# Seven-product sums in the words' own place, two word buffers, later transposes and four kept ring pieces

## The chip, the cores and the metric

The kernel runs on one core of a Trainium2 chip. The metric is the device time of one execution in microseconds (us). The engines of the core work side by side and wait for each other through semaphores: TensorE (PE; PEld is its weight load) multiplies matrices, VectorE (DVE) and ScalarE (ACT) do elementwise work, GpSimd (POOL) a little of it, and SyncE (SP) issues the loads from HBM in the order of one queue.

## The reference

An encoder of two layers works on 256 tokens of width 2048, all in fp32. Each layer adds a mixer and a gated feed-forward block (FFN), each followed by a layer norm:

```python
for layer in range(DEPTH):
    y = ab_mixer(...) if layer % 2 == 0 else cd_mixer(...)
    x = layer_norm(alpha * x + y, ...)
    y = (silu(x @ w_gate) * (x @ w_up)) @ w_down   # hidden width 5632
    x = layer_norm(alpha * x + y, ...)
```

Layer 0 mixes with a neighbourhood attention and a gated recurrence (`ab`), layer 1 with a multi-scale pool and a grouped-query attention (`cd`). Every mixer ends in an output projection. The change concerns the FFN and its borders.

## The kernel before

**Products.** An fp32 product is made of three matmuls in the faster F32R format (`mm3`, L261 to L266). Both factors are split into a high part and a remainder: ScalarE casts (`hi`, L122), VectorE subtracts (`lo`, L123). TensorE then adds low by high, high by high and high by low into one PSUM bank. Activations are split once and lie transposed (`xT`, `yT`); weights are split as they arrive. `load_half` (L143) loads 512 KB into one of four `raw` buffers; the split goes to a ring of `whi` and `wlo` buffers, which `open_ring` lengthens in some stages. A half feeds 12 matmuls of 512 columns: two token tiles, two rows of weights, three matmuls each.

**The FFN** (`ffn`, L462 to L527). The hidden width is 11 chunks of 512. Chunk 0 is made directly (`whole`). Chunks 1 to 10 are made by `unit`, in three phases that hold chunks 0 to 2, 3 to 6 and 7 to 10. Behind each phase the down projection of its chunks runs as four quarters `n`, and its result is added to the residual `res`.

**A unit** (L417 to L460) makes gate and up of one chunk from eight pairs of weight rows, in the order `PAIRS`. Five pairs are plain: two halves, 24 matmuls. Three (`SEVEN`: 5, 6, 7) use a seven-product scheme for the 2 by 2 block of token tiles and gate/up columns, 21 matmuls instead of 24. `load_seven` (L398) loads such a pair as one word of 1 MB (`rs`). From its four pieces come seven factors: three pieces are used as they are (cast L406, subtraction L410), four are sums, made in a tile `z` (L407 to L409) and split in their turn (L122, L123). `SEVEN_ORDER` gives the order of the seven products and the bank of each. The activations' counterparts are made once per layer by `forms_of` (`fs`, split into `fmh` and `fml`).

At the end of a unit ScalarE and VectorE combine the eight banks (L444 to L454), VectorE multiplies the gate by the up part into `g` (L458), and for each token tile TensorE transposes `g` (`transpose4`, L119), whose result is split into `yTh` and `yTl`: the down projection's left factor.

**PSUM** has eight banks. In the mixers they are "uses": three `acc`, two `tr` for transposes, three `mx`. In the FFN's units and first two down projections they are two "sides" of four, which change places from unit to unit.

**Order.** A scheduler sets the order of each engine's instructions from the program; `tc.high_priority` moves a block ahead by an offset. SP's loads go out in one queue's order, each as soon as its buffer is free. At the end of an FFN the norm runs with the last quarter of the down projection: `norm` scales `res` (L309), and `flip` transposes it for the next stage in pieces laid between the next stage's matmuls.

Of the kernel before, what the change touches and what calls it, by code (L numbers as in the profile page):

```python
# [11 lines left out]
F32 = mybir.dt.float32  # L12
# [6 lines left out]
P = 128  # L19
# [51 lines left out]
PAIRS = (0, 1, 5, 2, 3, 6, 4, 7)  # L71
SEVEN = (5, 6, 7)


@with_exitstack
def trunk(ctx: ExitStack, tc: tile.TileContext, a, out):
# [94 lines left out]

    def mm_chunk(halves, lhs, outs, tok_major=False, after=None, before=None):
# [32 lines left out]
        else:  # L205
            for i, (src, _) in enumerate(halves):
                loaded.append(load_half(src, before(i) if before else ()))
                for tok in range(NT):
                    mms(i, tok)
            if after:  # L210
# [36 lines left out]
    def transpose4(src, hi, lo):  # L247
# [4 lines left out]
        split(hi, lo, v)  # L252
# [19 lines left out]
    def residual_tools(res, gam, bet, betT):  # L272
        stats = [sm.tile([P, 4, 6], F32, tag=f"st{t}", name=f"st{t}", bufs=1) for t in range(NT)]
# [82 lines left out]
    def out_proj(w, order, groups, res, gb):  # L356
        evac, norm = residual_tools(res, *gb)
# [16 lines left out]
    def forms_of(sp, xT):  # L374
# [3 lines left out]
        xs = sp.tile([P, NT, 2 * n, P], F32, tag="rs", name="xs", bufs=1)  # L378
# [4 lines left out]
        fs = sp.tile([P, 4, n, P], F32, tag="z", name="fs", bufs=1)  # L383
# [14 lines left out]
    def load_seven(sp, src):  # L398

        with tc.high_priority(offset=400):  # L400
            raw = sp.tile([P, 4, NCH], F32, tag="rs", name="rs", bufs=1)
            hi = sp.tile([P, 7, NCH], F32R, tag="sh", name="sh", bufs=2)
            lo = sp.tile([P, 7, NCH], F32R, tag="sl", name="sl", bufs=2)
            z = sp.tile([P, 4, NCH], F32, tag="z", name="z", bufs=1)
            last_load[0] = nc.sync.dma_start(raw, src).ins
            nc.scalar.copy(hi[:, :3], raw[:, :3])  # L406
            nc.vector.tensor_tensor(z[:, :2], raw[:, 0:3:2], raw[:, 3:4].to_broadcast([P, 2, NCH]), op=add)  # L407
            nc.vector.tensor_tensor(z[:, 2], z[:, 0], raw[:, 2], op=add)
            nc.vector.tensor_tensor(z[:, 3], z[:, 2], raw[:, 1], op=add)  # L409
            nc.vector.tensor_tensor(lo[:, :3], raw[:, :3], hi[:, :3].bitcast(F32), op=sub)  # L410
            split(hi[:, 3:], lo[:, 3:], z)
# [3 lines left out]
    SEVEN_ORDER = ((0, "11", "p1"), (5, "f", "p6"), (3, "e", "p5"), (4, "g", "p7"), (1, "12", "c11"), (2, "h", "c12"), (6, "22", "c21"))  # L415

    def unit(sp, w, lhs, forms, yT):  # L417
# [8 lines left out]
        sevens = [p for p in PAIRS if p in SEVEN]  # L426
# [658 lines left out]
```

## Time and profile before

| what | value |
|---|---|
| median of 3 runs | 2236.31 us (2235.67 to 2237.08) |
| profiled execution | 2237.32 us |
| its span, first to last instruction | 2235.5 us |
| mean granted clock of TensorE | 0.988 |
| busy: PE, PEld, DVE, ACT | 98%, 81%, 73%, 48% |
| loaded and stored | 420.63 MB, 188 GB/s |

A share of busy time is a mean over stages. Matmuls are pipelined and overlap in the trace, so a busy PE is not PE at its peak. What a stage costs is read from TensorE's waits there and from the granted clock, which falls to half for some microseconds behind some of them.

### The profile page before, as it was taken

To read this page: it belongs to the slowest core of one execution; us is meant where nothing else is said; L and a number is where in the kernel's file an instruction comes from. 1 tells how busy PE (TensorE), PEld (TensorE's weight loads), DVE (VectorE), ACT (ScalarE), POOL (GpSimd) and SP (SyncE) were. 2 spreads that over 40 slices of the span, in tenths; PEclk is the share of its full clock that TensorE was granted. 3 is DMA by queue.
4 is the path that set the end of the run, shared out by engine and by line. 5 is a ranking of instruction groups with operands and counts; after the bars stand their busy time and mean duration, and the time that the engine had idled before them with its cause. 6 is when DMAs were issued, how large, how long until landed. Compare 5 with 4: busy or idle time off the path is not lost.

```text
span 2235.5 us, 26590 instructions
## 1 busy us (share of the span) xinstructions
PE 2183.4 (98%) x10000; PEld 1806.8 (81%) x10000; DVE 1636.4 (73%) x2016; ACT 1073.3 (48%) x1280; POOL 80.4 (4%) x67
## 2 busy tenths in 40 slices
PE   8999999999999999999999899999999999999997
PEld 7888888887778888888878688877778888888876
DVE  6886687566886788848876586675885789568865
ACT  6445544445453455544544564463544555345542
POOL 0010001002000000000000200020000000000001
PEclk9999999999999999999999999999999999999999
DMA  8555545664556555655557363654655556655553
GB/s 294 159 160 183 175 129 185 234 226 142 188 173 214 188 197 193 205 186 198 190 179 243 110 229 121 220 173 153 218 190 195 179 188 216 206 188 190 189 200 121
DMA packets 110257, 420.63 MB, mean 188 GB/s; under 512 B 13488, under 2 KB 16048, under 8 KB 101168
## 3 DMA queue, kind: packets, MB, share of 16 engines
q1 hardware_dynamic: 110128, 418.93, 56.0%
q8 instruction: 78, 1.28, 0.2%
q14 instruction: 51, 0.42, 0.1%
HBM read 416.78 MB, written 2.10 MB: 187 GB/s over the span
## 4 chain that ended last, share of the span: by engine, by line
PE 89%; DVE 6%; DMA 2%; issue 2%; ACT 1%; SPq 0%; POOL 0%; DVEq 0%; ACTq 0%; POOLq 0%
PE acc L264 39%; PE bside L264 25%; PE aside L264 21%; DVE wlo L123 2%; DMA rs<-in_gu 2%; PE mx L663 1%; PE mx L264 1%; PE tr L119 1%; DVE sl L410 1%; ACT whi L122 0%; PE aside L119 0%; PE bside L119 0%; DVE xTl L340 0%; ACT sh L406 0%; PE mx L709 0%
## 5 line engine op out<-in xcount | busy, mean ns | idle before, releaser
L123 DVE TENSOR_TENSOR wlo<-raw,whi 128x1024 fp32r<-128x1024 f32 (+1 forms) x641 | 787.6, 1238 | 383.5 <-ACT whi L122 379.2
L122 ACT CAST whi<-raw 128x1024 fp32r<-128x1024 f32 (+1 forms) x641 | 670.7, 1051 | 732.8 <-PE acc L264 266.1
L264 PE MATMUL acc<-whi,xTl 128*128 128x512 f32 x800 | 319.4, 400 | 14.4 <-DVE xTl L340 8.0
L264 PE MATMUL acc<-wlo,xTh 128*128 128x512 f32 x800 | 315.2, 396 | 5.1 <-DVE wlo L123 3.9
L264 PE MATMUL acc<-whi,xTh 128*128 128x512 f32 x800 | 317.1, 396 | 0.0
L264 PE MATMUL acc<-whi,yTl 128*128 128x512 f32 x512 | 201.3, 394 | 0.1
L264 PE MATMUL acc<-whi,yTh 128*128 128x512 f32 x512 | 200.7, 392 | 0.0
L264 PE MATMUL acc<-wlo,yTh 128*128 128x512 f32 x512 | 198.6, 391 | 0.0
L264 PEld LDWEIGHTS acc<-whi,xTl 128*128 128x128 f32 x800 | 152.4, 190 | 46.0 <-DVE xTl L340 8.5
L264 PEld LDWEIGHTS acc<-wlo,xTh 128*128 128x128 f32 x800 | 151.9, 190 | 39.0 <-DVE wlo L123 6.8
L264 PEld LDWEIGHTS acc<-whi,xTh 128*128 128x128 f32 x800 | 152.5, 191 | 29.1
L264 PE MATMUL bside<-whi,xTl 128*128 128x512 f32 x400 | 157.2, 394 | 1.4 <-DVE g L445 1.4
L264 PE MATMUL aside<-whi,xTl 128*128 128x512 f32 x400 | 156.0, 391 | 1.2 <-DVE yTl L123 1.2
L264 PE MATMUL bside<-whi,xTh 128*128 128x512 f32 x400 | 156.9, 392 | 0.0
L264 PE MATMUL aside<-whi,xTh 128*128 128x512 f32 x400 | 155.7, 389 | 0.0
L264 PE MATMUL bside<-wlo,xTh 128*128 128x512 f32 x400 | 153.5, 393 | 0.0
L264 PE MATMUL aside<-wlo,xTh 128*128 128x512 f32 x400 | 153.5, 390 | 0.0
L406 ACT CAST sh<-rs 128x1536 fp32r<-128x1536 f32 x60 | 89.0, 1484 | 131.9 <-DMA rs<-in_gu 77.7
L123 DVE TENSOR_TENSOR sl<-z,sh 128x2048 fp32r<-128x2048 f32 x60 | 137.3, 2288 | 20.6 <-ACT sh L122 19.5
L122 ACT CAST sh<-z 128x2048 fp32r<-128x2048 f32 x60 | 114.7, 1911 | 74.4 <-DVE z L409 74.4
L410 DVE TENSOR_TENSOR sl<-rs,sh 128x1536 fp32r<-128x1536 f32 x60 | 105.2, 1754 | 40.6 <-ACT sh L406 40.4
L264 PEld LDWEIGHTS acc<-wlo,yTh 128*128 128x128 f32 x512 | 96.8, 189 | 20.7 <-DVE wlo L123 0.5
(255 smaller groups left out, 3505.1 us busy)
## 6 DMA issues: line engine op xcount, KB each, us to landing
raw<-in_gu SPq DMA_DIRECT2D x232, 512.0 KB, 4.2
raw<-in_down SPq DMA_DIRECT2D x176, 512.0 KB, 4.2
raw<-in_ab_in SPq DMA_DIRECT2D x127, 512.0 KB, 4.2
rs<-in_gu SPq DMA_DIRECT2D x60, 1024.0 KB, 5.2
raw<-in_cd_in SPq DMA_DIRECT2D x40, 512.0 KB, 4.2
raw<-in_ab_out SPq DMA_DIRECT2D x32, 512.0 KB, 4.4
raw<-in_cd_out SPq DMA_DIRECT2D x32, 512.0 KB, 4.1
x<-in_xT SPq DMA_DIRECT2D x8, 256.0 KB, 6.4
```

Source lines behind the costliest of these rows:

```text
L119: return nc.tensor.transpose(o, src, eye)
L122: nc.scalar.copy(hi, src)
L123: nc.vector.tensor_tensor(lo, src, hi.bitcast(F32), op=sub)
L264: ins = nc.tensor.matmul(o, lhs[a], rhs[b], start=start and n == 0, stop=stop and n == 2)
L406: nc.scalar.copy(hi[:, :3], raw[:, :3])
L410: nc.vector.tensor_tensor(lo[:, :3], raw[:, :3], hi[:, :3].bitcast(F32), op=sub)
L663: nc.tensor.matmul(m[:, 2 * h + s, :], kk[:, h, s * P : (s + 1) * P], qq[:, h, r * P : (r + 1) * P], start=True, stop=True,)
```

## The change

1. In `load_seven` the first three pieces are split first, and then the sums overwrite the word itself (`raw`); the tile `z` is gone. The words have two buffers, which the forms use first (`xs`, `fs`). `SEVEN_ORDER` puts the three products of the first split ahead and the sixth (`f`) late.
2. Unit 1 takes its pairs in the order `PAIRS_FIRST`: four plain pairs ahead of the first word. Words have a lower priority in the first unit of each phase (`EARLY_FIRST`).
3. The product `g` and its transposes are no longer queued at the end of the unit: `later` holds each set of transposes, and `half_done` lets it go after two or three further halves, with the split at high priority. Behind unit 10 they go to `tr` banks within the down projection.
4. The end stage's ring of seven pieces becomes four and three. The four are `kept`: they stay through the `cd` mixer, in place of its own four (`wcd`), and into layer 1's output projection.
5. The norm's parameters are loaded behind the first quarter of the last down projection.

```diff
@@ -69,7 +69,11 @@
 PHASES = ((0, 1, 2), (3, 4, 5, 6), (7, 8, 9, 10))
 
 PAIRS = (0, 1, 5, 2, 3, 6, 4, 7)
+PAIRS_FIRST = (0, 1, 2, 3, 5, 4, 6, 7)
 SEVEN = (5, 6, 7)
+
+EARLY = 400
+EARLY_FIRST = 150
 
 
 @with_exitstack
@@ -169,6 +173,16 @@
     def two(k):
         return k, k + 1
 
+
+    later = []
+
+    def half_done(n=1):
+        for entry in list(later):
+            entry[0] -= n
+            if entry[0] <= 0:
+                later.remove(entry)
+                entry[1]()
+
     def mm_chunk(halves, lhs, outs, tok_major=False, after=None, before=None):
 
         n = len(halves)
@@ -207,6 +221,7 @@
                 loaded.append(load_half(src, before(i) if before else ()))
                 for tok in range(NT):
                     mms(i, tok)
+                half_done()
             if after:
                 for tok in range(NT):
                     after(tok)
@@ -244,12 +259,13 @@
         return f
 
 
-    def transpose4(src, hi, lo):
+    def transpose4(src, hi, lo, ahead_by=0):
         t = trp()
         for k in range(4):
             transpose(t[:, k * P : (k + 1) * P], src[:, k * P : (k + 1) * P], ident)
         v = t.rearrange("p (k t) -> p k t", k=4)
-        split(hi, lo, v)
+        with tc.high_priority(offset=ahead_by):
+            split(hi, lo, v)
 
     def split_tile(pool, shape, src, tag, bufs=1):
         hi = pool.tile(shape, F32R, tag=tag + "h", name=tag + "h", bufs=bufs)
@@ -269,8 +285,10 @@
         return pair[0][ix], pair[1][ix]
 
 
-    def residual_tools(res, gam, bet, betT):
-        stats = [sm.tile([P, 4, 6], F32, tag=f"st{t}", name=f"st{t}", bufs=1) for t in range(NT)]
+    def new_stats():
+        return [sm.tile([P, 4, 6], F32, tag=f"st{t}", name=f"st{t}", bufs=1) for t in range(NT)]
+
+    def residual_tools(res, gam, bet, betT, stats):
 
         def evac(tok, n, psum, start, last):
             r = res[tok][:, n * NCH : (n + 1) * NCH]
@@ -354,7 +372,7 @@
 
 
     def out_proj(w, order, groups, res, gb):
-        evac, norm = residual_tools(res, *gb)
+        evac, norm = residual_tools(res, *gb, new_stats())
         lhs = y_lhs(groups)
         xT = new_xT()
         for n in range(4):
@@ -375,12 +393,12 @@
 
         n = len(SEVEN)
         k = [slice(2 * SEVEN[0] + e, 2 * SEVEN[0] + 2 * n, 2) for e in range(2)]
-        xs = sp.tile([P, NT, 2 * n, P], F32, tag="rs", name="xs", bufs=1)
+        xs = sp.tile([P, NT, 2 * n, P], F32, tag="rs", name="xs", bufs=2)
         for t in range(NT):
             s = slice(2 * SEVEN[0], 2 * SEVEN[0] + 2 * n)
             nc.vector.tensor_tensor(xs[:, t], xT[0][t][:, s, :].bitcast(F32), xT[1][t][:, s, :].bitcast(F32), op=add)
         x11, x12, x21, x22 = (xs[:, t, e : 2 * n : 2, :] for t in range(2) for e in range(2))
-        fs = sp.tile([P, 4, n, P], F32, tag="z", name="fs", bufs=1)
+        fs = sp.tile([P, 4, n, P], F32, tag="rs", name="fs", bufs=2)
         e, f, g, h = (fs[:, i] for i in range(4))
         nc.vector.tensor_tensor(e, x22, x21, op=sub)
         nc.vector.tensor_tensor(f, e, x11, op=add)
@@ -395,26 +413,24 @@
             out.append({"11": x(0, k1), "12": x(0, k2), "22": x(1, k2), "e": e, "f": f, "g": g, "h": h})
         return dict(zip(SEVEN, out))
 
-    def load_seven(sp, src):
-
-        with tc.high_priority(offset=400):
-            raw = sp.tile([P, 4, NCH], F32, tag="rs", name="rs", bufs=1)
-            hi = sp.tile([P, 7, NCH], F32R, tag="sh", name="sh", bufs=2)
-            lo = sp.tile([P, 7, NCH], F32R, tag="sl", name="sl", bufs=2)
-            z = sp.tile([P, 4, NCH], F32, tag="z", name="z", bufs=1)
+    def load_seven(ss, sp, src, early):
+
+        with tc.high_priority(offset=early):
+            raw = sp.tile([P, 4, NCH], F32, tag="rs", name="rs", bufs=2)
+            hi = ss.tile([P, 7, NCH], F32R, tag="sh", name="sh", bufs=2)
+            lo = ss.tile([P, 7, NCH], F32R, tag="sl", name="sl", bufs=2)
             last_load[0] = nc.sync.dma_start(raw, src).ins
-            nc.scalar.copy(hi[:, :3], raw[:, :3])
-            nc.vector.tensor_tensor(z[:, :2], raw[:, 0:3:2], raw[:, 3:4].to_broadcast([P, 2, NCH]), op=add)
-            nc.vector.tensor_tensor(z[:, 2], z[:, 0], raw[:, 2], op=add)
-            nc.vector.tensor_tensor(z[:, 3], z[:, 2], raw[:, 1], op=add)
-            nc.vector.tensor_tensor(lo[:, :3], raw[:, :3], hi[:, :3].bitcast(F32), op=sub)
-            split(hi[:, 3:], lo[:, 3:], z)
+            split(hi[:, :3], lo[:, :3], raw[:, :3])
+            nc.vector.tensor_tensor(raw[:, 0:4:3], raw[:, 0:3:2], raw[:, 3:4].to_broadcast([P, 2, NCH]), op=add)
+            nc.vector.tensor_tensor(raw[:, 2], raw[:, 0], raw[:, 2], op=add)
+            nc.vector.tensor_tensor(raw[:, 1], raw[:, 2], raw[:, 1], op=add)
+            split(hi[:, 3:], lo[:, 3:], raw)
         return lambda i: (hi[:, i, :], lo[:, i, :])
 
 
-    SEVEN_ORDER = ((0, "11", "p1"), (5, "f", "p6"), (3, "e", "p5"), (4, "g", "p7"), (1, "12", "c11"), (2, "h", "c12"), (6, "22", "c21"))
-
-    def unit(sp, w, lhs, forms, yT):
+    SEVEN_ORDER = ((0, "11", "p1"), (1, "12", "c11"), (2, "h", "c12"), (3, "e", "p5"), (6, "g", "p7"), (5, "f", "p6"), (4, "22", "c21"))
+
+    def unit(ss, sp, pairs, w, lhs, forms, yT, opening):
 
         b = {n: side_bank() for n in ("c11", "c21", "c12", "c22")}
         begun = set()
@@ -423,13 +439,13 @@
             mm3(b[name], x, wt, name not in begun, last)
             begun.add(name)
 
-        sevens = [p for p in PAIRS if p in SEVEN]
-        plain = [p for p in PAIRS if p not in SEVEN]
-        for p in PAIRS:
+        sevens = [p for p in pairs if p in SEVEN]
+        plain = [p for p in pairs if p not in SEVEN]
+        for p in pairs:
             if p in SEVEN:
                 if p == sevens[0]:
                     b.update((n, side_bank(True)) for n in ("p1", "p6", "p5", "p7"))
-                wt = load_seven(sp, w[p])
+                wt = load_seven(ss, sp, w[p], EARLY_FIRST if opening else EARLY)
                 for i, x, name in SEVEN_ORDER:
                     product(name, forms[p][x], wt(i), p == sevens[-1])
             else:
@@ -439,6 +455,7 @@
                         for kk in range(2):
                             name = f"c{tok + 1}{n + 1}"
                             product(name, lhs(tok, ks[kk]), (hi[:, kk, :], lo[:, kk, :]), name == "c22" and p == plain[-1] and kk == 1)
+                    half_done()
         with tc.high_priority(offset=1000):
             g0, w_, v, x = (sp.tile([P, NCH], F32, tag=n, name=n, bufs=1) for n in ("g0", "g1", "u0", "u1"))
             nc.scalar.copy(g0, b["p1"])
@@ -457,9 +474,9 @@
             for tok, (g, u) in enumerate(((g0, v), (w_, x))):
                 nc.vector.tensor_tensor(g, g, u, op=mult)
                 s = slice(tok * P, (tok + 1) * P)
-                transpose4(g, yT[0][:, :, s], yT[1][:, :, s])
-
-    def ffn(layer, xT, res, mix_pool, close_mix, last):
+                later.append([2 + tok, lambda g=g, s=s: transpose4(g, yT[0][:, :, s], yT[1][:, :, s], 1000)])
+
+    def ffn(layer, xT, res, mix_pool, close_mix, keep, last):
         lhs = x_lhs(xT)
         w = a[f"gu{layer}"]
 
@@ -487,7 +504,7 @@
         groups = {0: whole(0, mix_pool, True)}
         close_mix()
         stack = ExitStack()
-        sp = later_pool(stack, f"s{layer}")
+        ss, sp = later_pool(stack, f"ss{layer}"), later_pool(stack, f"sp{layer}")
         open_banks("sides")
         with tc.high_priority(offset=2000):
             forms = forms_of(sp, xT)
@@ -497,19 +514,20 @@
             for c in chunks:
                 if c not in groups:
                     groups[c] = new_yT()
-                    unit(sp, w[c], lhs, forms, groups[c])
+                    unit(ss, sp, PAIRS_FIRST if c == 1 else PAIRS, w[c], lhs, forms, groups[c], c - 1 in (0, *(p[0] - 1 for p in PHASES)))
             gl = [groups[c] for c in chunks]
             if end:
                 stack.close()
                 open_banks("uses")
-                open_ring(later_pool(stack, f"er{layer}"), 7)
-                fp = later_pool(stack, f"e{layer}")
-                gb = load_gb(fp, layer, "ffn")
+                open_ring(keep(f"er{layer}"), 4)
+                open_ring(later_pool(stack, f"e{layer}"), 3)
+                fp = later_pool(stack, f"g{layer}")
                 nxt = None if last else new_xT()
-                evac, norm = residual_tools(res, *gb)
-            else:
-                evac, _ = residual_tools(res, None, None, None)
+            stats = new_stats()
+            evac, norm = residual_tools(res, None, None, None, stats)
             for n in range(4):
+                if end and n == 1:
+                    evac, norm = residual_tools(res, *load_gb(fp, layer, "ffn"), stats)
                 outs = [acc() for _ in range(NT)]
                 halves = [(a[f"down{layer}"][n, 2 * c + i], two(4 * ci + 2 * i)) for ci, c in enumerate(chunks) for i in range(2)]
 
@@ -522,8 +540,9 @@
                 mm_chunk(halves, y_lhs(gl), outs, tok_major=(end and n == 3), after=after)
             if not end:
                 banks["side"] ^= 1
-        rings.pop()
-        stack.close()
+        if end:
+            rings.pop()
+            stack.close()
         return nxt
 
 
@@ -947,27 +966,32 @@
     def later_pool(stack, name):
         return stack.enter_context(tc.tile_pool(name=name, bufs=1, reuse_waits="tile"))
 
+
+    kept = ExitStack()
+
+    def keep(name):
+        return later_pool(kept, name)
+
     def layer_end(i, w, groups, yT, last):
 
         stack = ExitStack()
-        open_ring(later_pool(stack, f"fr{i}"), 7)
+        open_ring(later_pool(stack, f"fr{i}"), 7 - 4 * i)
         fp = later_pool(stack, f"f{i}")
 
         def close():
-            rings.pop()
+            del rings[1:]
             stack.close()
+            kept.close()
 
         xT = out_proj(w, groups, yT, res, load_gb(fp, i, "mix"))
-        return ffn(i, xT, res, fp, close, last)
+        return ffn(i, xT, res, fp, close, keep, last)
 
     xT = layer_end(0, a["ab_out"], AB_OUT_GROUPS, yT, False)
     yT = [new_yT() for _ in range(4)]
-    with tc.tile_pool(name="wcd", bufs=1, reuse_waits="tile") as wcd:
-        rings.append((wcd, 4))
-        with tc.tile_pool(name="cd", bufs=1, reuse_waits="tile") as mp:
-            cd_mixer(mp, xT, yT)
-    rings.pop()
+    with tc.tile_pool(name="cd", bufs=1, reuse_waits="tile") as mp:
+        cd_mixer(mp, xT, yT)
     layer_end(1, a["cd_out"], CD_OUT_GROUPS, yT, True)
+    kept.close()
 
 
 
```

The new line numbers: `split` is L126 and L127, `mm3` L280, the transposes L123, the sums L424 to L426, the combination at a unit's end L461 to L475. Three places show how the instructions move.

SP, layer 0's FFN, from chunk 0 into units 1 and 2 (`raw` are halves, `rs` the words). Before:

```order
L159 DMA raw<-in_gu 128x1024 x24
L405 DMA rs<-in_gu 128x2048
L159 DMA raw<-in_gu 128x1024
L405 DMA rs<-in_gu 128x2048
L159 DMA raw<-in_gu 128x1024 x3
L405 DMA rs<-in_gu 128x2048
L159 DMA raw<-in_gu 128x1024 x4
L405 DMA rs<-in_gu 128x2048
L159 DMA raw<-in_gu 128x1024 x2
L405 DMA rs<-in_gu 128x2048
L159 DMA raw<-in_gu 128x1024 x2
L159 DMA raw<-in_down 128x1024 x3
```

Now:

```order
L163 DMA raw<-in_gu 128x1024 x24
L422 DMA rs<-in_gu 128x2048 x2
L163 DMA raw<-in_gu 128x1024 x5
L422 DMA rs<-in_gu 128x2048
L163 DMA raw<-in_gu 128x1024
L422 DMA rs<-in_gu 128x2048
L163 DMA raw<-in_gu 128x1024 x4
L422 DMA rs<-in_gu 128x2048 x2
L163 DMA raw<-in_gu 128x1024 x2
L163 DMA raw<-in_down 128x1024 x3
L422 DMA rs<-in_gu 128x2048
L163 DMA raw<-in_down 128x1024 x5
```

The first two words go out together, and five halves follow before the third; two pairs of words stand together where there were single ones.

TensorE, layer 0, from the last matmuls of unit 10 (`aside`, `bside`) to the last down projection (`acc`). Before:

```order
L264 MATMUL bside<-sh,xTh_3815 128x512
L264 MATMUL bside<-sl,xTh_3815 128x512
L119 MATMUL bside<-ident,g_9104 128x128 x4
L119 MATMUL bside<-ident,g_9105 128x128 x4
L264 MATMUL acc<-whi,yTl 128x512
L264 MATMUL acc<-whi,yTh 128x512
L264 MATMUL acc<-wlo,yTh 128x512
L264 MATMUL acc<-whi,yTl 128x512
```

Now, the same border, and then the place of the first set of transposes:

```order
L280 MATMUL bside<-sh,xTh_3815 128x512
L280 MATMUL aside<-sl,fmh 128x512 x3
L280 MATMUL bside<-sl,xTh_3815 128x512
L280 MATMUL acc<-whi,yTl 128x512
L280 MATMUL acc<-whi,yTh 128x512
L280 MATMUL acc<-wlo,yTh 128x512
L280 MATMUL acc<-whi,yTl 128x512
```

```order
L280 MATMUL acc<-whi,yTl 128x512
L280 MATMUL acc<-whi,yTh 128x512
L280 MATMUL acc<-wlo,yTh 128x512
L123 MATMUL tr<-ident,g_9077 128x128 x4
L280 MATMUL acc<-whi,yTl 128x512
L280 MATMUL acc<-whi,yTh 128x512
L280 MATMUL acc<-wlo,yTh 128x512
```

The transposes have moved from between the two stages to behind 24 matmuls of the second, into a `tr` bank; the second set follows 12 matmuls later.

ScalarE, layer 0, from the last down projection (the first row holds its halves) into the norm (`res`), the flips (`xTh`) and the first halves of the `cd` projection. Before:

```order
L122 CAST whi<-raw 128x1024 x28
L309 ACTIVATE res_3796<-res_3796,rstd 128x512 x4
L338 ACTIVATE xTh_9152<-tr,betT 128x128 x4
L338 ACTIVATE xTh_9152<-mx,betT 128x128 x4
L122 CAST whi<-raw 128x1024 x2
L338 ACTIVATE xTh_9152<-tr,betT 128x128 x4
L338 ACTIVATE xTh_9152<-mx,betT 128x128 x4
L122 CAST whi<-raw 128x1024 x2
L309 ACTIVATE res_3797<-res_3797,rstd 128x512 x3
```

Now:

```order
L126 CAST whi<-raw 128x1024 x28
L327 ACTIVATE res_3796<-res_3796,rstd 128x512 x4
L126 CAST whi<-raw 128x1024
L356 ACTIVATE xTh_9109<-tr,betT 128x128 x4
L126 CAST whi<-raw 128x1024
L356 ACTIVATE xTh_9109<-mx,betT 128x128 x4
L356 ACTIVATE xTh_9109<-tr,betT 128x128 x4
L126 CAST whi<-raw 128x1024
L356 ACTIVATE xTh_9109<-mx,betT 128x128 x4
L126 CAST whi<-raw 128x1024
L327 ACTIVATE res_3797<-res_3797,rstd 128x512 x3
```

Counted from the kernel's start, 365 casts of halves stand ahead of the first `res` row before and 368 now; so three of the next projection's halves come ahead of the norm where none did.

## Rows read from the trace of the kernel before

**Rows 1.** Waits of TensorE, whole span: engine, tile, releaser: us in total, times, longest.
```profile
PE bside L119 <- DVE g L458: 6.5, 5, 1.8
PE aside L264 <- DVE wlo L123: 4.5, 2, 3.4
```

**Rows 2.** Windows: length, busy us of PE, PEld, DVE, ACT, POOL, granted clock, DMA share, GB/s.
```profile
528.00:536.00 8.00, 8.00 (x29) 6.48 (x30) 4.16 (x16) 1.14 (x2) 0.00 (x0) 0.80 0.26 89
613.00:621.00 8.00, 7.30 (x20) 5.71 (x20) 8.00 (x12) 5.46 (x5) 0.00 (x0) 0.57 0.36 132
671.00:679.00 8.00, 6.93 (x21) 5.29 (x20) 6.64 (x8) 3.43 (x3) 0.00 (x0) 0.57 0.87 283
1158.00:1166.00 8.00, 6.67 (x28) 5.44 (x27) 3.47 (x6) 2.74 (x4) 0.00 (x0) 0.79 0.43 173
1258.00:1266.00 8.00, 6.55 (x21) 4.66 (x20) 4.73 (x7) 4.94 (x7) 0.63 (x1) 0.57 0.61 179
...
1680.00:2125.00 445.00, 445.00 (x1991) 368.39 (x1990) 337.81 (x325) 217.03 (x200) 0.00 (x0) 1.00 0.57 193
```

**Rows 3.** Waits of TensorE from 560 to 625 us (units 1 and 2, layer 0).
```profile
PE bside L264 <- DVE sl L410: 2.0, 2, 1.1
PE bside L264 <- ACT sh L406: 0.8, 1, 0.8
```

**Rows 4.** Timeline of TensorE there: start, duration, instruction, idle before and its releaser.
```profile
577.71 0.50 PE L264 MATMUL bside<-sl,xTh 128*128 128x512 f32 x1 [0.98 <-DVE sl L410]
```

**Rows 5.** Timeline of VectorE there.
```profile
569.60 1.76 DVE L123 TENSOR_TENSOR fml<-fs,fmh 128x1536 fp32r<-128x1536 f32 x1 [1.55 <-ACT fmh L122]
```

**Rows 6.** The chain that ended last: a word's load, start and us to landing.
```profile
600.85 8.38 DMA rs<-in_gu
```

**Rows 7.** DMA issues of the whole span: count, KB each, median us to landing.
```profile
rs<-in_gu SPq DMA_DIRECT2D x60, 1024.0 KB, 5.2
```

**Rows 8.** Instruction groups of the whole span: busy us, mean ns, idle before.
```profile
L123 DVE TENSOR_TENSOR wlo<-raw,whi 128x1024 fp32r<-128x1024 f32 (+1 forms) x641 | 787.6, 1238 | 383.5 <-ACT whi L122 379.2
...
L406 ACT CAST sh<-rs 128x1536 fp32r<-128x1536 f32 x60 | 89.0, 1484 | 131.9 <-DMA rs<-in_gu 77.7
...
L410 DVE TENSOR_TENSOR sl<-rs,sh 128x1536 fp32r<-128x1536 f32 x60 | 105.2, 1754 | 40.6 <-ACT sh L406 40.4
...
L407 DVE TENSOR_TENSOR z<-rs 128x1024 f32<-128x1024 f32 x60 | 73.2, 1220 | 29.2 <-DMA rs<-in_gu 29.0
L408 DVE TENSOR_TENSOR z<-z,rs 128x512 f32<-128x512 f32 x60 | 41.0, 684 | 0.2
```

**Rows 9.** Waits of TensorE from 640 to 682 us (unit 2 to the down projection, layer 0).
```profile
PE aside L264 <- ACT whi L122: 1.9, 1, 1.9
PE aside L264 <- DVE wlo L123: 1.1, 1, 1.1
```

**Rows 10.** Timeline of TensorE at the end of unit 10, layer 0.
```profile
1153.74 0.39 PE L264 MATMUL bside<-sh,xTl 128*128 128x512 f32 x1
...
1155.55 0.39 PE L264 MATMUL bside<-sl,xTh 128*128 128x512 f32 x1
1157.78 0.66 PE L119 MATMUL bside<-ident,g 128*128 128x128 f32 x4 [1.84 <-DVE g L458]
1159.77 1.11 PE L119 MATMUL bside<-ident,g 128*128 128x128 f32 x4 [1.33 <-DVE g L458]
```

**Rows 11.** Timeline of ScalarE at the end of layer 0.
```profile
1248.06 2.01 ACT L122 CAST whi<-raw 128x1024 fp32r<-128x1024 f32 x2
```

**Rows 12.** Waits of TensorE from 1240 to 1276 us (end of layer 0).
```profile
PE acc L264 <- DVE wlo L123: 3.9, 6, 1.4
PE acc L264 <- DVE rstd L218: 1.2, 1, 1.2
PE acc L264 <- ACT whi L122: 0.8, 1, 0.8
```

**Rows 13.** Waits of TensorE from 515 to 533 us (output projection to FFN, layer 0).
```profile
PE acc L264 <- DVE xTl L340: 4.0, 1, 4.0
```

## The prediction

> **What bounds the kernel now.** I began with the windows, because the bound must be known stage by stage. In a long stretch of layer 1's units (the last line of [rows 2]) TensorE is busy for all 445.00 us at full clock, and VectorE for 337.81 of them (76%). Nothing that merely lightens VectorE or the queues can gain there: TensorE runs its matmuls back to back, and one 512-column matmul starts every 0.227 us (eight steps in the 1.81 us between the first two lines of [rows 10]). The kernel computes the same matmuls after the change, so only the places where TensorE waits can change the time, plus new waits.
>
> The waits on TensorE [rows 1] name those places, and windows of 8 us [rows 2] show the second half of each price: after a cluster of waits the granted clock drops. A window of 8 us with a mean of 0.57 lost 0.43 x 8 = 3.4 us at half speed (1.2 instead of 2.4 GHz), one of 0.79 lost 1.7 us. I price a place as its matmul waits plus this loss. Five kinds of place concern the change:
>
> - A: layer 0's first two units. Waits 2.0 + 0.8 [rows 3] and 3.4 of clock: 6.2 us. Readers should see that the releasers are the split of the seven-product words, and that VectorE is busy 8.00 of 8 us there [rows 2].
> - B: layer 0's step from unit 2 to the down projection. Waits 1.9 + 1.1 [rows 9] and 3.4: 6.4 us. The releasers are the cast and the subtraction of plain halves.
> - C: layer 1's first phase. One wait of 3.4 us for a half's subtraction [rows 1]; with a clock loss like B's, an estimate of 6.8 us.
> - D: unit 10 to the last down projection, once per layer. TensorE's two sets of transposes wait 1.84 and 1.33 us for the product `g` [rows 10], and 1.7 of clock follow: 4.9 us. The line for `g` in [rows 1] holds 6.5 us, so both layers pay it.
> - E: end of layer 0 to the projection of the next mixer. Waits 3.9 + 1.2 + 0.8 [rows 12] and 3.4 of clock: 9.3 us.
>
> **The change, part by part.** *Transposes queued later (D).* Before, both sets of transposes stand in TensorE's queue between the last product and the down projection, behind a VectorE chain that ends only after the unit. The new order puts 24 matmuls (5.4 us) ahead of the first set and 36 (8.2 us) ahead of the second. The last product starts at 1155.55 and the second set had its data by 1159.77, 4.2 us later [rows 10], so both are ready in time. What is late next is PSUM: the down projection's first bank held the sixth product, which ends one matmul before the unit does, and its reader is one VectorE operation of 0.68 us [rows 8]; the second bank is wanted six matmuls later and read two such operations later. I allow 0.8 + 0.3 = 1.1 us, with bounds of 0 (banks free in time) and 3.2 (today's wait); so short a wait should bring no clock loss. Gain 4.9 - 1.1 = 3.8 us per layer, 7.6 together. In mid-phase the transposes already had the next unit's matmuls around them; I count nothing there. Their cover is those matmuls: without them they would cost D's price.
>
> *Four pieces' room outlives the layer (E).* ScalarE casts the next mixer's first two halves only at 1248.06, behind the norm and half of its transposes [rows 11]. In the new order three casts stand ahead of the norm, so their `raw` buffers come free earlier and the following loads go out earlier. The norm and its transposes keep their own cost. The nearest rows for that are the same code at layer 0's mixer end, where the next weights are already split: one wait of 4.0 us [rows 13] and 0.20 x 8 = 1.6 us of clock (the first line of [rows 2]), 5.6 us. So 9.3 - 5.6 = 3.7 us gained. Bounds: 0, if TensorE still runs out of halves, and 5.9, the waits of [rows 12] all gone and the clock loss of 3.4 left.
>
> *Words in two buffers, first word later (A).* In unit 1 the first word is now needed after four plain pairs (96 matmuls, 21.8 us) instead of two (48, 10.9 us). So the wait that ended at 577.71 [rows 4] goes. Both first words are issued back to back; the second reuses the buffer of the forms, so it waits for `fml`, which ends at 571.4 [rows 5]. Next is the seventh half (pair 3): its subtraction stands in VectorE's new order behind the second word's first split. TensorE wants it 72 matmuls into the unit: 577.71 - 0.98 - 10.9 + 16.3 = 582.1. With the median load of 5.2 us [rows 7] the word lands at 576.6; cast 1.48, split 1.75, one sum of 0.68 and the half's own 1.24 [rows 8] give 581.8, in time. With 8.38 us, which a word took behind queued halves [rows 6], it is 584.9: 2.8 us late. I take 1.0, nearer to the 5.2 since at that point no halves are issued ahead of it.
> [...]
> Pair 7's word now waits for a buffer that is free only when the whole in-place chain of pair 5 has ended, and three splits and sums stand among the first evacuation's operations. I allow 2.4 us more for these, between 0 and the 5.2 that would leave A at its present 6.2. A goes from 6.2 to 3.4, a gain of 2.8.
>
> *Sums in place.* The same count and shapes of additions, so nothing on VectorE's total. But the sums must now wait for the first split, which reads the same words: cast 1.48 and subtraction 1.75 [rows 8] are in series with them, 3.24 us more from landing to last split. Cover: only the first three words of seven are needed by the first nine matmuls, and loads run ahead by a pair. If that cover is gone, see the slower rival.
>
> *B and C.* Transposes move between halves here too, which helps; but two first splits and a sum (1.75 + 1.75 + 1.22 = 4.7 us by [rows 8]) stand ahead of the third half of the down projection on VectorE, which is busy 6.64 of 8 us there [rows 2]. The gain lies between 6.4 + 6.8 (both vanish) and -4.7 in each; I take 0, since TensorE has only four split halves of cover and both directions have a row.
>
> *Edits with no cost.* The parameter loads of 1 MB that move behind the first quarter of the down projection are wanted only at its end; `new_stats` and the ring's split into 4 + 3 change no instruction; SP issues as many loads as before.
>
> **Sum.** 2.8 + 0 + 0 + 7.6 + 3.7 = 14.1 us. The profiled execution took 2237.3 us, hence 2223.2; it stands 1.0 above the median of the runs, so 2222.2.
>
> **The rivals.** *More vanishes.* If VectorE's new order also suffices in A, B and C, 3.4 + 6.4 + 6.8 = 16.6 us more go: 2205.6. For it: the splits that released the waits come earlier in the order, and B's halves no longer follow the transposes' split. Against: VectorE has no free time in those stretches [rows 2].
> *It doesn't do what it says at the ends.* If the down projection's banks come free only when the evacuation chain is through, TensorE waits at the bank instead of at the transposes and D keeps its 4.9 us: 2222.2 + 7.6 = 2229.8. For it: the same operations read these banks. Against: the order of reads puts the needed banks first.
> *Given back.* The first unit of each phase gets two word loads and two first splits at once. If B and C each become worse by their bound of 4.7 and A by 2.8 + 2.4 (the half late by all of 2.8, the word buffer double), 14.6 us go back: 2236.8, no change.
> *Slower.* One mechanism: the longer chain in every unit. A word buffer is now held 3.24 us longer, and words stand in pairs ahead of plain halves in SP's order; [rows 6] show a 1 MB load taking 8.38 us behind halves against 5.2 [rows 7], and the reverse is as likely. If in each of the 20 units one product waits 1.2 us, 24 us come on: 2246. It decides from the point where the lead of a word (a pair's 24 matmuls, 5.4 us, and more) is less than 3.24 plus the 3.2 us by which a crowded load is late: 6.4 us. Against: in [rows 2] the units run with no wait at all and VectorE has 24% free.
> On this the Trainium skill ("DMA: Bandwidth & Descriptors", section Queues, rings and completion order) says that each DMA engine takes one queue's descriptors in the order of the ring, so halves would queue behind the pair of words; the 8.38 us agrees with that for the opposite order.
>
> **How the numbers follow.** Chances: forecast 0.51, more vanishes 0.17, no effect at the ends 0.08, given back 0.12, slower 0.12. About 0.2%, 4.5 us, is what a measurement of this kernel can tell from no change. Faster by more: 0.51 + 0.17 + 0.08 = 0.76; within: 0.12; slower: 0.12. The range starts at 2204, the rival with more gain, and reaches to 2240, past the case given back; it leaves out the slower rival and gains beyond C's estimate.
>
> **What would show it.** Right: at unit 10's end the down projection's matmuls follow the last product with about 1 us of wait and the clock stays at 1.00; the next mixer's first casts lie before the norm's; in unit 1 the waits on the word's split are gone. Wrong: a repeated TensorE wait on `sl` or `wlo` within units of the later phases; waits at B or C above 5 us; `tr` transposes that still wait for `g`.

## The result and the profile after

The change is slower: a median of 2248.55 us (2245.71 to 2251.05, 4 runs) against 2236.69 us for the kernel before beside it (2235.67 to 2240.14, 4 runs). The ratio is 1.005, 95% interval 1.0032 to 1.0067. I had forecast 2222.2, faster, in a range of 2204 to 2240: wrong in direction and outside the range.

The profiled execution took 2245.71 us, its span is 2243.9 us, 8.4 longer than before. The mean granted clock rose from 0.988 to 0.993 all the same. To see where the time went, I took for every matmul of the trace the distance to the next start, less the median distance of its kind. The sum of this excess is 77.0 us before and 84.7 after, which accounts for 7.7 of the 8.4 us (it holds waits and time at the half clock alike):

| place | excess before, us | after, us |
|---|---|---|
| D: unit 10 to the last down projection, layers 0 and 1 | 5.0 + 5.3 | 1.4 + 1.4 |
| E: end of layer 0 to the `cd` projection | 11.6 | 2.3 |
| A: units 1 and 2, layer 0 | 7.5 | 5.4 |
| B: unit 2 to the down projection, layer 0 | 6.6 | 9.3 |
| C: the same two stretches in layer 1 | 7.9 | 12.1 |
| borders of units 5 to 6 and 9 to 10, both layers | 0 | 4.4 + 4.3 + 4.4 + 4.3 |
| all else | 33.1 | 35.4 |

So the borders that the change was to mend gave 16.8 us back (D and E), and the words took more than that. The last place but one was on no list of mine. At the first of these borders, from 845 to 866 us, TensorE waits as follows (us in total, times, longest); the window has its columns as in [rows 2]:

```profile
PE aside L280 <- DVE g L462: 1.6, 1, 1.6
PE aside L280 <- ACT sh L126: 1.2, 1, 1.2
PE aside L280 <- ACT g L461: 0.2, 1, 0.2
PE aside L280 <- DVE sl L127: 0.2, 1, 0.2
```
```profile
845.00:866.00 21.00, 17.73 (x75) 13.40 (x74) 17.47 (x17) 9.27 (x7) 0.00 (x0) 1.00 0.38 136
```

In the kernel before the same window reads:

```profile
845.00:866.00 21.00, 21.00 (x94) 17.41 (x93) 19.14 (x20) 10.68 (x11) 0.00 (x0) 1.00 0.49 165
```

The timelines of VectorE, which subtracts and adds, and of ScalarE, which casts, say why. After the change, at the end of unit 5, VectorE:

```profile
847.12 3.43 DVE L127 TENSOR_TENSOR sl<-rs,sh 128x1536 fp32r<-128x1536 f32 x2 [3.92 <-ACT sh L126]
850.47 1.22 DVE L424 TENSOR_TENSOR rs<-rs 128x1024 f32<-128x1024 f32 x1
851.60 1.22 DVE L127 TENSOR_TENSOR wlo<-raw,whi 128x1024 fp32r<-128x1024 f32 x1
852.74 1.22 DVE L424 TENSOR_TENSOR rs<-rs 128x1024 f32<-128x1024 f32 x1
...
856.21 1.29 DVE L426 TENSOR_TENSOR rs<-rs 128x512 f32<-128x512 f32 x2
858.87 4.49 DVE L127 TENSOR_TENSOR sl<-rs,sh 128x2048 fp32r<-128x2048 f32 x2 [1.37 <-ACT sh L126]
863.28 0.68 DVE L462 TENSOR_TENSOR g<-g,aside 128x512 f32<-128x512 f32 x1
```

And ScalarE, whose first cast waits for a matmul (`PE aside`), not for a load:

```profile
845.61 2.86 ACT L126 CAST sh<-rs 128x1536 fp32r<-128x1536 f32 x2 [3.66 <-PE aside L280]
...
856.93 3.71 ACT L126 CAST sh<-rs 128x2048 fp32r<-128x2048 f32 x2 [3.03 <-DVE rs L426]
```

Before, ScalarE and VectorE:

```profile
841.10 1.48 ACT L406 CAST sh<-rs 128x1536 fp32r<-128x1536 f32 x1 [0.76 <-PE aside L264]
```
```profile
835.50 0.67 DVE L409 TENSOR_TENSOR z<-z,rs 128x512 f32<-128x512 f32 x1
...
842.61 1.76 DVE L410 TENSOR_TENSOR sl<-rs,sh 128x1536 fp32r<-128x1536 f32 x1 [1.01 <-ACT sh L406]
844.42 2.29 DVE L123 TENSOR_TENSOR sl<-z,sh 128x2048 fp32r<-128x2048 f32 x1
...
854.26 0.68 DVE L445 TENSOR_TENSOR g<-g,aside 128x512 f32<-128x512 f32 x1
...
858.45 2.28 DVE L123 TENSOR_TENSOR sl<-z,sh 128x2048 fp32r<-128x2048 f32 x1
```

Before, the sums of pair 7's word stood ready in `z` (the last of them at 835.50) when its factor buffer, the pair of `sh` and `sl` that its splits write, came free. So its last split (844.42) followed the first (842.61) at once. Now the sums wait for the first split, and the first split for the factor buffer, which pair 5's last product still reads. Two words are in this state together, pair 7's of unit 5 and the first of unit 6: each operation comes twice (the "x2" rows). I call this the lockstep. From the start of the first split to the end of the pair of last splits it takes 16.2 us (847.12 to 863.3), where pair 7's word alone took 4.1 before (842.61 to 846.71); TensorE waits 1.2 us for its cast. The unit's evacuation, the operations that combine its eight banks (L462 is VectorE's first), stands behind both splits and so frees its bank 1.6 us too late.

The ends of the stages are as they were meant to be. TensorE at the end of unit 10, to compare with [rows 10], and the window there: no transposes between the stages, and no drop of the clock.

```profile
1165.63 0.39 PE L280 MATMUL bside<-sl,xTh 128*128 128x512 f32 x1
1166.64 0.51 PE L280 MATMUL acc<-whi,yTl 128*128 128x512 f32 x1 [0.62 <-DVE g L462]
...
1172.78 0.60 PE L123 MATMUL tr<-ident,g 128*128 128x128 f32 x4
```
```profile
1164.00:1172.00 8.00, 7.13 (x30) 5.24 (x30) 6.04 (x11) 1.70 (x3) 0.00 (x0) 1.00 0.42 133
```

At the end of layer 0 ScalarE casts three halves ahead of the norm, the first at 1232.99, where [rows 11] have 1248.06; of the waits in [rows 12] 1.5 us are left (waits of TensorE from 1225 to 1276 us):

```profile
1232.99 1.05 ACT L126 CAST whi<-raw 128x1024 fp32r<-128x1024 f32 x1 [4.96 <-DMA raw<-in_cd_in]
1238.64 1.05 ACT L126 CAST whi<-raw 128x1024 fp32r<-128x1024 f32 x1 [4.59 <-DMA raw<-in_cd_in]
1247.15 1.05 ACT L126 CAST whi<-raw 128x1024 fp32r<-128x1024 f32 x1 [7.46 <-PE acc L280]
1248.11 2.56 ACT L327 ACTIVATE res<-res,rstd 128x512 f32<-128x512 f32 x4
```
```profile
PE tr L123 <- ACT res L327: 1.2, 1, 1.2
PE acc L280 <- DVE wlo L127: 0.3, 1, 0.3
```

### The profile page after: what moved, and what is told of

Its sections match the earlier page's. It is cut to its first block, busy times and chain, and to the rows that moved or that the text cites. A ratio compares the mean times of both kernels' runs of the same rounds, so it can differ in the third digit from the quotient of the medians.

```text
span 2243.9 us, 26478 instructions
## 1 busy us (share of the span) xinstructions
PE 2180.1 (97%) x10000; PEld 1799.7 (80%) x10000; DVE 1638.6 (73%) x2016; ACT 1072.3 (48%) x1280; POOL 82.1 (4%) x67
## 4 chain that ended last, share of the span: by engine, by line
PE 87%; DVE 8%; issue 2%; ACT 2%; DMA 1%; POOL 0%; DVEq 0%; ACTq 0%; POOLq 0%
PE acc L280 38%; PE bside L280 24%; PE aside L280 20%; DVE wlo L127 2%; DVE sl L127 2%; PE mx L682 1%; ACT sh L126 1%; DMA rs<-in_gu 1%; PE mx L280 1%; DVE rs L424 1%; PE tr L123 1%; DVE rs L425 1%; DVE xTl L358 0%; PE aside L123 0%; ACT whi L126 0%
## 5 line engine op out<-in xcount | busy, mean ns | idle before, releaser
L127 DVE TENSOR_TENSOR wlo<-raw,whi 128x1024 fp32r<-128x1024 f32 (+1 forms) x641 | 790.6, 1241 | 374.1 <-ACT whi L126 368.5
L126 ACT CAST whi<-raw 128x1024 fp32r<-128x1024 f32 (+1 forms) x641 | 670.7, 1051 | 723.8 <-PE acc L280 253.0
L280 PE MATMUL acc<-whi,xTl 128*128 128x512 f32 x800 | 318.5, 399 | 13.9 <-DVE xTl L358 8.0
L280 PE MATMUL acc<-whi,xTh 128*128 128x512 f32 x800 | 316.7, 396 | 0.0
L280 PE MATMUL acc<-wlo,xTh 128*128 128x512 f32 x800 | 314.1, 395 | 0.3 <-DVE wlo L127 0.3
L127 DVE TENSOR_TENSOR sl<-rs,sh 128x1536 fp32r<-128x1536 f32 (+1 forms) x120 | 241.5, 2023 | 98.4 <-ACT sh L126 98.1
L126 ACT CAST sh<-rs 128x1536 fp32r<-128x1536 f32 (+1 forms) x120 | 201.1, 1695 | 221.7 <-DVE rs L426 80.1
L280 PE MATMUL acc<-whi,yTl 128*128 128x512 f32 x512 | 201.2, 394 | 1.9 <-DVE g L462 1.2
L280 PE MATMUL acc<-whi,yTh 128*128 128x512 f32 x512 | 199.9, 390 | 0.0
L280 PE MATMUL acc<-wlo,yTh 128*128 128x512 f32 x512 | 198.0, 390 | 0.0
L280 PEld LDWEIGHTS acc<-whi,xTl 128*128 128x128 f32 x800 | 152.0, 190 | 44.0 <-DVE xTl L358 8.5
L280 PEld LDWEIGHTS acc<-wlo,xTh 128*128 128x128 f32 x800 | 151.7, 190 | 31.6 <-DVE wlo L127 1.0
L280 PEld LDWEIGHTS acc<-whi,xTh 128*128 128x128 f32 x800 | 152.1, 190 | 29.0
L280 PE MATMUL bside<-whi,xTl 128*128 128x512 f32 x400 | 157.5, 394 | 4.4 <-DVE g L462 4.0
L280 PE MATMUL aside<-whi,xTl 128*128 128x512 f32 x400 | 156.8, 392 | 4.8 <-DVE g L462 3.2
L280 PE MATMUL bside<-whi,xTh 128*128 128x512 f32 x400 | 156.3, 391 | 0.0
L280 PE MATMUL aside<-whi,xTh 128*128 128x512 f32 x400 | 155.9, 390 | 0.0
L280 PE MATMUL aside<-wlo,xTh 128*128 128x512 f32 x400 | 153.8, 391 | 0.7 <-DVE wlo L127 0.7
L280 PE MATMUL bside<-wlo,xTh 128*128 128x512 f32 x400 | 152.7, 392 | 0.0
L280 PEld LDWEIGHTS acc<-whi,yTl 128*128 128x128 f32 x512 | 96.2, 188 | 23.1 <-DVE g L462 2.1
L280 PEld LDWEIGHTS acc<-wlo,yTh 128*128 128x128 f32 x512 | 96.2, 188 | 20.3 <-DVE wlo L127 0.5
L280 PEld LDWEIGHTS acc<-whi,yTh 128*128 128x128 f32 x512 | 96.3, 188 | 19.3
```

The lines of the kernel that those rows point to most:

```text
L126: nc.scalar.copy(hi, src)
L127: nc.vector.tensor_tensor(lo, src, hi.bitcast(F32), op=sub)
L280: ins = nc.tensor.matmul(o, lhs[a], rhs[b], start=start and n == 0, stop=stop and n == 2)
```

## The experiments

The kernel before was run beside each group of runs (1 to 4, 5 to 8, 9 to 11); a ratio is to its runs there. Its own median lay between 2236.69 and 2240.99 us from group to group, so a difference between runs of two groups is uncertain by some 4 us. The code edits are cut to their main lines.

**1. The two borders alone.** From the kernel before: only unit 10's transposes are deferred, and `er` is kept as in the change; words, sums and orders stay.

```diff
-                transpose4(g, yT[0][:, :, s], yT[1][:, :, s])
+                if defer:
+                    later.append([2 + tok, lambda g=g, s=s: transpose4(g, yT[0][:, :, s], yT[1][:, :, s], 1000)])
+                else:
+                    transpose4(g, yT[0][:, :, s], yT[1][:, :, s])
```

> The kernel before, with only the two border parts of the change: unit 10's transposes inside the last down projection (with the parameter loads behind its first quarter), and four ring pieces kept through the next mixer. Words, sums, order of pairs and of products, and the mid-phase transposes are those of before. My theory (the borders gained, the words lost): the trace of the change lost 1.4 us at each unit-10 border where before lost 5.0 and 5.3, and 2.3 at the end of layer 0 where before lost 11.6, 16.7 us together; so 2236.7 - 16.7 = 2220. Rival (the borders gained only because other stretches were late, or shift their loss): within 4.5 us of before, 2232 to 2241.

Measured: 2220.55 us, ratio 0.9918 (0.9889 to 0.9947). The gain of the two borders together is real and stands without the rest. It beats both kernels.

**2. The sums apart again.** From the change, which includes the new order of products; the sums write `z` again and stand ahead of the first split's subtraction.

```diff
-            raw = sp.tile([P, 4, NCH], F32, tag="rs", name="rs", bufs=2)
+            raw = sp.tile([P, 4, NCH], F32, tag="rs", name="rs", bufs=1)
+            z = sp.tile([P, 4, NCH], F32, tag="z", name="z", bufs=1)
```

> The change, with the sums back in a tile of their own, one word buffer, and the sums ahead of the first split's subtraction; all else as in the change. My theory (the longer chain of two words in place is what lost): the waits of 3.9 + 0.5 us at the borders from unit 5 to 6 and from 9 to 10 in both layers go (17.4 us), and some of the 7 us more at the ends of both first phases: 2222 to 2231. Rival (the later transposes lost): 2245 to 2252, as the change.

Measured: 2226.18 us, ratio 0.9942 (0.9925 to 0.9959): 22 us less than the change. In its trace one wait is left from 800 to 900 us, of 0.3 us. So with the new order of products the words in place, with their second buffer, cost what the borders gave, and more.

**3. Mid-phase transposes queued at the unit's end again.** From the change.

> The change, but the transposes of all units except unit 10 are queued at the unit's end as before. Rival theory (transposes that are queued two and three halves later hold the banks of the next unit's pair 5, so pair 7's word finds its factor buffer late): 17 us faster than the change, near 2231. My theory (the transposes are late because the product g is late on VectorE, behind the splits of two words): the order of the instructions hardly differs, so 2245 to 2252, no difference.

Measured: 2248.97 us, ratio 1.004 (1.0025 to 1.0055), as the change. The order of TensorE's instructions shows it too: in unit 5 the second set of transposes stands behind 111 matmuls in both, so the later queueing moves nothing there.

**4. The words alone.** From the kernel before: sums in place, two buffers, new order of products.

> The kernel before, with only the words changed: sums in place behind the first split, two word buffers, the new order of the seven products. My theory: the border waits of the change appear without its other parts: 17 us at the borders from unit 5 to 6 and 9 to 10, perhaps less at others, so 2247 to 2262. Rival (the parts hurt only together, for example by the lower priority of words in opening units): 2233 to 2241.

Measured: 2268.09 us, ratio 1.0133 (1.0107 to 1.0159), worse than I expected. From 840 to 862 us TensorE's waits are, to the tenth, those that the change has from 845 to 866. At the end of unit 10, where nothing defers the transposes here, they wait up to 4.3 us for `g` instead of 1.84 [rows 10]:

```profile
PE bside L119 <- DVE g L456: 5.2, 2, 4.3
```

**5. The new order of products alone**, with the sums apart.

```diff
-    SEVEN_ORDER = ((0, "11", "p1"), (5, "f", "p6"), (3, "e", "p5"), (4, "g", "p7"), (1, "12", "c11"), (2, "h", "c12"), (6, "22", "c21"))
+    SEVEN_ORDER = ((0, "11", "p1"), (1, "12", "c11"), (2, "h", "c12"), (3, "e", "p5"), (4, "g", "p7"), (5, "f", "p6"), (6, "22", "c21"))
```

> The kernel before, with only the new order of the seven products (sums still in a tile of their own). Theory that the in-place chain lost: no difference, within 0.3% of the kernel before run beside it, and no wait on sh or g at the borders of units 5 to 6 and 9 to 10. Rival (the late sixth product frees its bank late, whence the waits on g there): 1.6 us and more at each border, at least 0.4% slower.

Measured: 2244.51 us, ratio 1.0022 (1.0005 to 1.004). The number lies within the 0.3% of my theory, and from 840 to 866 us TensorE has no wait, so the rival's waits at those borders don't come. But the order does cost some 5 us (1 to 9 by the interval), and not at nothing as I had thought: in this trace TensorE's waits for `g` at the transposes sum to 11.8 us, against 6.5 in [rows 1].

```profile
PE bside L119 <- DVE g L458: 11.8, 6, 3.9
```

VectorE's first operation of the evacuation reads the bank of `p6`. It started 2.3 us before the unit's last product before the change (1153.26 against 1155.55); in the new order `p6` is the last but one, and at the end of unit 10 VectorE idles for it, and TensorE's transposes for `g`:

```profile
1151.35 0.69 DVE L445 TENSOR_TENSOR g<-g,aside 128x512 f32<-128x512 f32 x1 [2.02 <-PE aside L264]
```
```profile
1155.81 0.65 PE L119 MATMUL bside<-ident,g 128*128 128x128 f32 x4 [3.89 <-DVE g L458]
```

**6. The words in place, old order of products.** From run 4.

> The words in place with two buffers as in the run of the words alone, but with the old order of the products. Theory that the in-place chain lost: still slower than before by 15 us or more, since the splits of pair 7 and of the next unit's first word still come together; perhaps slower than with the new order, since the second product needs a sum. Rival (the new order lost): within 5 us of before.

Measured: 2246.16 us, ratio 1.0026 (1.001 to 1.0041). My number was wrong: of the 27 us of run 4 the old order takes 20 away. At the border of units 5 and 6 the lockstep is still there and one wait of 1.4 us for the bank with it, but the wait for the cast is gone. The new order by itself cost 5 us (run 5), the words in place by themselves 7, both together 27 (run 4): together more than their sum.

**7. One word buffer.** From run 4, `bufs=1`.

> The words in place with the new order, but one word buffer. If the 10 us chain in itself lost: as slow as with two buffers or slower (27 us over before), with waits on sh or sl in most units. If two words in lockstep lost, which only the second buffer allows: the waits of 3.9 + 0.5 us at the borders go and the time is within 10 us of before.

Measured: 2380.19 us, ratio 1.0627 (1.0599 to 1.0655). The chain in place needs the second buffer. With one, TensorE waits 32 times for a word's cast:

```profile
PE aside L264 <- ACT sh L122: 42.2, 16, 3.8
PE bside L264 <- ACT sh L122: 39.4, 16, 4.0
```

Where unit 6 of layer 0 ends, for example, it waits 2.71 us for a word's last cast and then 3.75 us for the first cast of the next word, whose load is issued only at 922.05, when the chain before it has ended.

**8. The two borders, and all transposes queued later.** From run 1.

> The version with the two border parts alone, and now all transposes queued two and three halves later, as in the change. Theory (the later queueing in mid-phase does nothing, for the order hardly changes): within 3 us of the version with the border parts alone, 20 us under before. Rival (it holds banks of the next unit): 5 us or more slower than that version.

Measured: 2214.95 us, ratio 0.9889 (0.9861 to 0.9916). Its interval overlaps that of run 1, so the later queueing in mid-phase is not shown to do anything. Its median is the lowest of all versions.

**9. One word at a time on VectorE.** From the change. The order of the engine is held, no instruction is added.

```diff
+                for ins in words_end:
+                    order.enter_context(tc.issue_after(ins))
+                nc.vector.tensor_tensor(lo[:, :3], raw[:, :3], hi[:, :3].bitcast(F32), op=sub)
```

> The change, with one rule more: on VectorE a word's first split and sums are issued only behind the last split of the word before it. Same instructions. Theory (pair 7's word and the next unit's first word run in lockstep on VectorE, so that both last splits stand together ahead of the unit's evacuation): the waits of 3.9 + 0.5 us at the borders of units 5 to 6 and 9 to 10 go in both layers, 17 us, and the ends of the first phases gain some too: 2220 to 2233. Rival (the length of one word's chain, 10 us, or the factor buffer that is free late): no gain or slower, 2243 to 2260.

Measured: 2237.96 us, ratio 0.9999 (0.9986 to 1.0012): 11 us less than the change, though not the 15 to 28 that I expected. That the lockstep made the border waits is shown: from 720 to 890 us no wait of TensorE is left, and VectorE reaches the last split of pair 7 before the next word's first:

```profile
846.92 1.76 DVE L429 TENSOR_TENSOR sl<-rs,sh 128x1536 fp32r<-128x1536 f32 x1
...
854.14 2.29 DVE L434 TENSOR_TENSOR sl<-rs,sh 128x2048 fp32r<-128x2048 f32 x1 [2.75 <-ACT sh L433]
856.35 1.75 DVE L429 TENSOR_TENSOR sl<-rs,sh 128x1536 fp32r<-128x1536 f32 x1
```

A part comes back as longer waits elsewhere: 3.4 us instead of 1.0 from 890 to 930 us, where unit 6 meets the down projection, 3.3 instead of 2.0 us for a cast in unit 1, and 4.4 instead of 2.7 for a half's subtraction behind unit 2. The first of these places:

```profile
PE bside L280 <- DVE wlo L127: 2.7, 2, 1.5
PE bside L280 <- ACT sh L433: 0.7, 1, 0.7
```

**10. The change with the old order of products.**

> The change with the old order of the seven products. By the runs of the words alone, 2268 with the new order and 2246 with the old one, the border waits fall from 4.3 to 1.6 us each: 11 us at four borders and some at the first phases' ends, so 2228 to 2240. If the new order is needed with unit 1's new order of pairs or with the later transposes: 2244 or more.

Measured: 2235.72 us, ratio 0.999 (0.9976 to 1.0004). The new order costs the change about 13 us. At the border of units 5 and 6 one wait of 1.4 us for the bank is left, as in run 6.

**11. One word at a time and the old order.**

> One word at a time and the old order of the products, otherwise the change. If lockstep is the cause, the order matters little once it is broken: within 6 us of the run with one word at a time in the new order. If the order is a cause of its own (its second product needs a sum): 6 us or more apart from that run.

Measured: 2225.97 us, ratio 0.9942 (0.992 to 0.9965), 12 us under run 9. So the order is a cause of its own also without lockstep. Two places show it: at the end of unit 10 the waits for the banks, 0.6 + 0.3 us in run 9, are gone, and behind unit 2 the wait for a half's subtraction is 1.3 us instead of 4.4. With both undone, the sums in place come out at the time of run 2, which has the sums apart but still the new order. Run 8, with neither the words in place nor the new order, is another 11 us faster.

## Why the prediction was wrong

*The sum of the table.* The places A to E gave 12.0 us, where I had 14.1. The miss is in what the sum had at nothing: the four unit borders, 17.4 us, and 2.3 us elsewhere.

*D* was right, in the mechanism and in size: 7.5 us gained, 7.6 forecast. It left 0.6 + 0.2 us of waits where I allowed 1.1, for the bank's reader that I had named, with no loss of clock. *E* had the right mechanism and the wrong size: it gave 9.3 us, where I took 3.7 and set a bound of 5.9. I priced what remains by [rows 13] with their loss of clock, and here neither the wait of 4.0 nor the loss came. Run 1 shows the two terms together, without the rest.

*A* was near, 2.1 us gained against 2.8, in part by luck. The half of pair 3 waited 0.7 us (I took 1.0), and a word and the bank 2.0 + 0.4 (I took 2.4). But the 2.0 us are for a word's last cast, which itself waited for the last sum in place (L426), and the clock still fell once there (0.79 in the window from 606 to 614 us), which I hadn't priced. The second word came in as by the 5.2 us of [rows 7]: its cast began at 576.90, and I had it landing at 576.6.

*The step that failed* is "Sums in place", which I put at nothing. I counted 3.24 us more from landing to last split and took the lead of a load as its cover. With the new order of products it cost 17.4 us at the four borders; with the old order one wait of 1.4 us is left where I looked, from unit 5 to 6 (runs 6 and 10). The chain doesn't start at landing. The first split writes into a factor buffer that is free only when pair 5's last product is done. Before, the sums needed no factor buffer and were made while it was held; now they are behind it. In the new order of TensorE in unit 5, pair 5's last product is number 147 and pair 7's first number 174: 27 matmuls, 6.1 us at 0.227, against 41 (129 and 170), 9.3 us, before. The chain in place takes 10 us: its casts, splits and sums take 1.48, 1.76, 1.23, 0.69, 0.69, 1.90 and 2.29 in the trace. One chain by itself still comes in time at these borders, for run 9 has no wait there. Two at once don't: the first of the two last casts is done at about 858.8, 13 us after the first cast began, and TensorE has waited 1.2 us for it. Run 2 undoes the sums in place and wins 22 us. I had the numbers of these matmuls in the order before the run, and looked only at the queues around the stages' borders.

*"Transposes later ... I count nothing there"* was right (run 3). *The new order of products* I listed but priced only as bringing the first split's products forward. It costs 5 us by itself (run 5) and 13 in the change (run 10): I didn't follow it to `p6`, the first bank that VectorE's evacuation reads. That the bank is the cause is shown at the end of unit 10 (run 5); for the rest of the 13 us it is not.

*B and C* I put at 0 between bounds; they lost 2.7 and 4.2 us, within them. In "given back" I counted the late half's 2.8 us on top of the 1.0 that A already held; that sum is 13.6, so 2235.8.

*The slower rival* named the right part, the chain in place, with a chance of 0.12, but another mechanism: a late load, and 1.2 us in each of 20 units. No load is late where it stalls. The loss sits in four borders of 4.4 us and at the ends of the first phases. That its 2246 lies near the measured 2248.55 is luck.

*"VectorE has 24% free"* was the argument that misled me. It says that VectorE can do its work in time, not that it does it in the right order. In the window of the stall it is free for 3.5 of 21 us and TensorE waits for it.

What stays open: why order and words in place together cost more than their sum; the longer waits in run 9 in unit 1 and behind units 2 and 6 were not taken apart; and no run takes unit 1's order of pairs and the lower priority of words alone. Runs 2 and 11 still have both, run 8 has neither and is 11 us faster than either, so a part of that may be theirs.

## What to carry to other kernels

When an operation is moved into a buffer that its input occupies, ask which resource the first reader of that input waits for: the whole chain now begins there, not at the landing of the data. When a step's products change places, look which bank is read first behind it. And test the parts of a mixed change one by one: here two gave 17 us or more, and two took it away.

## What was not expected of the hardware

The clock did not follow the length of the waits. At the border of units 5 and 6, waits of 1.2, 0.2 and 1.6 us within 7 us left the granted clock at 1.00 (window above, and on to 890 us), while 1.84 and 1.33 us at the end of unit 10 were followed by 0.79 in the kernel before [rows 2, 10]. The two places differ in what TensorE did between the waits: at the border twelve matmuls of 512 columns between the first and the last, at the end of unit 10 only four transposes of 128 columns. No run here shows whether that decides. In the change the drops at the end of unit 10 and of layer 0 are gone with their waits (both windows read 1.00, against 0.79 and 0.57 before), and the new waits at the borders bring none. So it has the higher mean clock, 0.993 against 0.988, and the longer time.
